# Spreading queries and keys ahead of the next raw weights in a hybrid decoder layer, with three weight splits moved

## The chip, the cores and the metric

The kernel runs on one core of a Trainium2 chip. The metric is device time in microseconds (us) for one execution of the whole layer. TensorE is called PE, VectorE DVE, ScalarE ACT, GpSimd POOL and SyncE SP, as in the profile. Before the change the median of 3 runs is 604.84 us (604.68 to 605.78).

## What is computed

One decoder layer on 512 tokens with 1024 channels, float32 throughout. The input projection feeds a pooling mixer (u) and block-sparse attention with 8 heads of 64 (q, k, v); then the output projection, a gated MLP with a short convolution, and an embedding gate:

```python
h = rms_norm(x, g_mix_pre[i])
proj = h @ w_in[i]
u, q, k, v = jnp.split(proj, [D_POOL, D_POOL + D_ATTN, D_POOL + 2 * D_ATTN], axis=-1)
y_pool = pool_mixer(u, w_pool[i], pool_scale[i])
y_attn = moba_attention(q, k, v, rel_bias)       # heads split off; own block and past blocks
y = jnp.concatenate([y_pool, y_attn], axis=-1) @ w_out[i]
x = x + rms_norm(y, g_mix_post[i])
h = rms_norm(x, g_ffn_pre[i])
x = x + rms_norm(conv_ffn(h, w_up[i], conv_w[i], conv_b[i], w_down[i]), g_ffn_post[i])
x = x + (p[i] @ w_ple[i]) * jax.nn.sigmoid(x @ w_ple_gate[i])
```

With 512 tokens, blocks of 256 and three past blocks to choose, every query sees all earlier keys, so the kernel computes plain causal attention.

## The kernel before

Every float32 product is made of three matmuls (`mm3`, lines 224 to 226) on operands that are split into a high and a low part: low times high, high times low, high times high. A weight therefore passes through four steps in the class `_Weights`. SP loads a chunk of 1 MB into one of two raw buffers (`load`, lines 110 and 118). A chunk holds two pieces; for each piece ACT casts the high part (`wh`, line 147) and DVE subtracts it from the raw data (`wl`, line 148). `W.ahead(n)` puts the splits of the next pieces into the program at the place where it is called, until n pieces beyond those already used are split. As soon as both pieces of a chunk are split, the load of the chunk two further on is put into SP's queue at that place.

The pieces in the order of their use: 0 to 3 the value weights, 4 and 5 the query weights of the first two pairs of heads (q0, q1), 6 and 7 their key weights (k0, k1), 8 and 9 pooling inputs u0 and u1, 10 to 13 q2, k2, q3, k3, 14 and 15 u2 and u3, 16 to 23 the output projection W_out. Chunk c holds the pieces 2c and 2c + 1.

`project` makes one projection of 24 matmuls and then calls `W.ahead(n)`. `query(hp)` projects the queries of a pair of heads and writes the high and low parts (lines 415 and 416) into the buffer `QK`. `key(hp)` does so for the keys (lines 229 and 230, the helper `split`). From `QK`, SP copies both parts into the operands of two single heads, `ST[0]` and `ST[1]`, in the trace the tiles q and k: four transfers of 128 KB for the queries (line 427) and four of 256 KB for the keys (line 434), two for each head. The next pair's projection can be written into `QK` only when these have landed. PE's scores of a head (line 444) need that head's q and k.

The attention is a hand-written order over the heads h = 0 to 6. For each h the program puts out one or two projections that fill PE (`fills`), then `transposes(h)` of the softmaxed scores L (line 471, evicted by ACT and DVE as `PT`), `scores(h + 1)` with the softmax of that head on DVE and ACT (lines 450 to 456, the last step being four multiplications on line 456), the copies of the next pair, and `values(h)` (line 491, whose result is taken from the bank that the first of the head's transposes used, and is evicted on lines 496 to 500). After head 6 PE makes parts of the output projection, `out_part(0, 0, ...)`, the tile y, with the input rows in the order 4, 5, 0, 1, 6, which are in the pieces 18, 18, 16, 16, 19. Then follow the transposes of head 7.

Every engine works through its instructions in program order, so the place of a call of `W.ahead` decides what waits behind a split on ACT and DVE and behind a load in SP's queue. The pooling inputs are summed on POOL (lines 512 to 518) beside the heads 0, 1, 5 and 6.

Of the kernel before, what the change touches and what calls it, by code (L numbers as in the profile page):

```python
# [17 lines left out]
F32 = mybir.dt.float32  # L18
# [12 lines left out]
H = 8  # L31
DH = 64
# [130 lines left out]
def hybrid_layer(ctx, tc, x, p, rel_bias, g_mix_pre, g_mix_post, g_ffn_pre, g_ffn_post, w_in, w_pool,  # L163
                 pool_scale, w_out, w_up, conv_w, conv_b, w_down, w_ple, w_ple_gate, onehot, out):
    nc = tc.nc
    act, dve, pool, pe, sp = nc.scalar, nc.vector, nc.gpsimd, nc.tensor, nc.sync
# [10 lines left out]
    def bank(name, tag="mm"):  # L177
        return psum.tile([P, 512], F32, tag=tag, name=name, bufs=banks[tag])


    W = _Weights(nc, wts)
# [33 lines left out]
    for i in GATE:  # L215
        if i in (1, 2, 3):
            row, n = {1: (0, 0), 2: (KG, 0), 3: (KG, 1)}[i]
# [4 lines left out]
    def mm3(o, st, mv, first, last, more=False):  # L222

        pe.matmul(o, st[1], mv[0], start=first, stop=False, skip_group_check=more)  # L224
        pe.matmul(o, st[0], mv[1], start=False, stop=False, skip_group_check=more)  # L225
        pe.matmul(o, st[0], mv[0], start=False, stop=last, skip_group_check=more)  # L226

    def split(pair, src):
        act.copy(pair[0], src)
        dve.tensor_sub(pair[1], src, pair[0].bitcast(F32))  # L230
# [37 lines left out]
    def h_moving(k, half=None):  # L268
        part = slice(0, NT) if half is None else slice(2 * half, 2 * half + 2)
        return [q[:, part, k, :] for q in hT]  # L270
# [104 lines left out]
    ps = bank("rows", "pt")  # L375
# [23 lines left out]
    def project(name, tag="mm", n=3):  # L399
        w = W.take()  # L400
        ps = bank(name, tag)
        for k in range(KD):
            mm3(ps, [q[:, k, :] for q in w], h_moving(k), k == 0, k == KD - 1)
        W.ahead(n)
        return ps
# [4 lines left out]
    QK = ap2.tile([P, 4, S], F32R, name="qk")  # L410
    ST = [[ap2.tile([P, S], F32R, name=f"q_{e}"), ap2.tile([P, 2, S], F32R, name=f"k_{e}")] for e in range(2)]

    def query(hp):
        ps = project(f"q{hp}")
        act.mul(QK[:, 0, :], ps, -(DH ** -0.5))
        dve.scalar_tensor_tensor(QK[:, 3, :], ps, -(DH ** -0.5), QK[:, 0, :].bitcast(F32), op0=ALU.mult,
                                 op1=ALU.subtract)

    def key(hp):
        ps = project(f"k{hp}")  # L420
        split([QK[:, 1, :], QK[:, 2, :]], ps)

    def spread_queries():

        for e in range(2):
            for a in range(2):
                sp.dma_start(ST[e][0][a * DH:(a + 1) * DH].bitcast(F32),
                             QK[e * DH:(e + 1) * DH, 0 if a == e else 3, :].bitcast(F32))

    def spread_keys():  # L430

        for e in range(2):
            for a in range(2):
                sp.dma_start(ST[e][1][a * DH:(a + 1) * DH].bitcast(F32), QK[e * DH:(e + 1) * DH, 1:3, :].bitcast(F32))

    place = {3: (0, 0, 768), 2: (1, 0, 384), 0: (1, 384, 0), 1: (2, 0, 128)}

# [38 lines left out]
    def moving(q, j):  # L476
        if j < 3:
            o = (P, P + 512, P + 896)[j]
            return q[:, o:o + (NT - j) * P]
        return q.rearrange("p (a b) -> p a b", b=P)[:, 0::10, :]  # L480

    def values(h):
        hp, e = divmod(h, 2)
        ps = bank(f"o{h}", "pt")
        for c in range(2):
            for j in range(NT):
                o = ps[:, min(j, 2) * P:]
                if j == 3:
                    o = o.rearrange("p (a b) -> p a b", b=P)
                w = V[:, j, hp, e].rearrange("p a d -> p (a d)")  # L490
                pe.matmul(o, w, moving(PT[c], j), start=j == 0 and c == 0, stop=j == NT - 1 and c == 1)  # L491
        rows = slice(e * DH, (e + 1) * DH)
        other = slice((1 - e) * DH, (2 - e) * DH)
        hi, lo = (q[rows, 4 + hp, :] for q in yT)
        t = ap2.tile([P, S], F32, tag="t", name=f"t{h}", bufs=1)
        act.copy(t[rows, :], ps[other, :])
        act.copy(hi, ps[rows, :])
        d = ap2.tile([P, S], F32, tag="d", name=f"d{h}", bufs=1)
        dve.tensor_sub(d[rows, :], ps[rows, :], hi.bitcast(F32))
        dve.tensor_add(lo, d[rows, :], t[rows, :])  # L500
# [3 lines left out]
    def pool_in(g):  # L504

        w = 2 << g
        ps = project(f"u{g}", n=4 if g == 3 else 3)
        act.copy(ub[0][:, 16:], ps)  # L508
        src = ub[0]
        for lvl in range(g + 1):  # L510
            nxt = ub[1 + lvl % 2]
            pool.tensor_tensor(out=nxt[:, 16:], in0=src[:, 16:], in1=src[:, 16 - (1 << lvl):16 + S - (1 << lvl)],  # L512
                               op=ALU.add)
            src = nxt
        pool.tensor_tensor(out=src[:, 16:16 + w], in0=src[:, 16:16 + w], in1=inv_count[:, :w], op=ALU.mult)
        pool.tensor_scalar(src[:, 16 + w:], src[:, 16 + w:], 1.0 / w, None, op0=ALU.mult)
        pooled[g] = ap2.tile([P, S], F32, tag="pd", name=f"pd{g}", bufs=2)
        pool.tensor_tensor(out=pooled[g], in0=src[:, 16:], in1=ub[0][:, 16:], op=ALU.subtract)
# [6 lines left out]
    def pool_out(g, tag="mm"):  # L525
        mp = bank(f"mix{g}", tag)
        mm3(mp, [q[:, g, :] for q in wp], pooled[g], True, True)
        act.mul(yT[0][:, g, :], mp, pscale[:, g:g + 1])
        dve.scalar_tensor_tensor(yT[1][:, g, :], mp, pscale[:, g:g + 1], yT[0][:, g, :].bitcast(F32),
                                 op0=ALU.mult, op1=ALU.subtract)  # L530
# [4 lines left out]
    def y_stationary(t, k):  # L535
        return [q[:, k, t * P:(t + 1) * P] for q in yT]

    yb = {}
    part = (4, 5, 0, 1, 6)
    query(0)  # L540
    spread_queries()
    query(1)
    key(0)
    spread_keys()
    key(1)
    split(wp, wpool)
    scores(0)
    fills = {0: [lambda: pool_in(0)], 1: [lambda: pool_in(1)],
             2: [lambda: query(2), lambda: pool_out(0)],
             3: [lambda: key(2), spread_keys, lambda: query(3), lambda: pool_out(1)],  # L550
             4: [lambda: key(3)], 5: [lambda: pool_in(2)],
             6: [lambda: pool_in(3)]}
    after = {1: lambda: pool_mid(0), 2: lambda: pool_mid(1), 6: lambda: pool_mid(2)}
    for h in range(H - 1):
        for f in fills[h]:
            f()
        transposes(h)
        scores(h + 1)
        if h in (0, 2, 4):
            spread_queries()  # L560
            if h != 2:
                spread_keys()
        values(h)
        if h in after:
            after[h]()

# [76 lines left out]
    for k in range(2):  # L643
        ps = bank(f"trp{k}", "pt")
# [137 lines left out]
    u = 0  # L782
    for fb in range(1, NF // 2):
        for post in (gate_post, value_post):
            for f in (2 * fb, 2 * fb + 1):
                ps = project(f"{post.__name__[:4]}{f}", tags[u % 5])
# [5 lines left out]
                else:  # L792
                    k, step = divmod(u - 2 * NK, 3)
# [36 lines left out]
    for g, (i, ks) in enumerate(GROUPS):  # L830
        m_next()
        w = W.take()
# [238 lines left out]
```

## Time and profile before

| | |
|---|---|
| median of 3 runs | 604.84 us |
| the profiled execution, its own time | 605.41 us |
| its span from first to last instruction | 603.6 us |
| PE busy | 588.9 us, 98% of the span |
| DVE, ACT, POOL busy | 424.0, 292.6, 234.8 us |
| PE's share of the chain that ended last | 92% |
| mean granted PE clock | 0.99 of full speed |

In the page's 40 slices of 15.1 us PE is busy in nine tenths or more of all but a few. The exceptions that lie in the attention are one slice of six tenths near 68 us, with a granted clock of seven tenths, and one of eight tenths near 143 us, with a clock of eight tenths. The list of PE's waits and the timelines around these two places tell what PE waited for.

### The profile page before, as it was taken

How to read it: one execution, taken by the hardware profiler on the slowest of the kernel's cores; microseconds unless marked ns; L12 is line 12 of the kernel's file. 1: busy time of each engine (PE TensorE's matmuls, PEld its weight loads, DVE VectorE, ACT ScalarE, POOL GpSimd, SP SyncE). 2: the span in 40 equal slices, each digit the busy share in tenths (PEclk: the TensorE clock that was granted, in tenths of full speed). 3: DMA queues.
4: the chain of work that ended last, by engine and by line, in shares of the span. 5: the costliest groups of instructions: out<-in, count | busy, mean ns of one | idle time of the engine just before them, and what ended most of it. 6: DMA issues, size and time to landing. Idle time of an engine off the chain costs nothing.

```text
span 603.6 us, 7483 instructions
## 1 busy us (share of the span) xinstructions
PE 588.9 (98%) x2752; PEld 489.5 (81%) x2752; DVE 424.0 (70%) x556; ACT 292.6 (48%) x476; POOL 234.8 (39%) x236
## 2 busy tenths in 40 slices
PE   9999699998999999999999999999999999999996
PEld 5887588887888998888888888888888878888885
DVE  4643278688468857868656658868787686878985
ACT  6432267566264534425334334444646565866461
POOL 2300050037213739998820787584240000012930
PEclk9999799998999999999999999999999999999999
DMA  8676563551642297998972565786655575752974
GB/s 296 199 268 181 130 175 104 157 159 69 245 139 71 79 390 269 344 356 287 375 269 69 210 208 210 259 287 218 206 170 185 191 270 184 262 193 72 346 242 176
DMA packets 68012, 128.57 MB, mean 213 GB/s; under 512 B 4115, under 2 KB 35439, under 8 KB 66568
## 3 DMA queue, kind: packets, MB, share of 16 engines
q1 hardware_dynamic: 58392, 88.69, 45.3%
q0 software_dynamic: 9584, 39.41, 17.3%
q8 instruction: 21, 0.34, 0.2%
q14 instruction: 15, 0.12, 0.1%
HBM read 97.65 MB, written 26.76 MB: 206 GB/s over the span
## 4 chain that ended last, share of the span: by engine, by line
PE 92%; DVE 2%; DMA 2%; ACT 1%; issue 1%; SPq 0%; POOL 0%; DVEq 0%; ACTq 0%; POOLq 0%
PE gate L224 6%; PE valu L224 6%; PE gate L226 6%; PE valu L226 6%; PE gate L225 6%; PE valu L225 6%; PE d L224 6%; PE d L226 5%; PE d L225 5%; PE y L226 2%; PE y L224 2%; PE y L225 2%; PE g L226 2%; PE g L225 2%; PE g L224 2%; PE o L491 2%
## 5 line engine op out<-in xcount | busy, mean ns | idle before, releaser
L148 DVE TENSOR_TENSOR wl<-raw,wh 128x1024 fp32r<-128x1024 f32 (+1 forms) x118 | 156.9, 1336 | 23.1 <-ACT wh L147 22.6
L147 ACT CAST wh<-raw 128x1024 fp32r<-128x1024 f32 (+1 forms) x118 | 118.7, 1021 | 23.4 <-DMA raw<-in_w_up 7.1
L741 POOL TENSOR_TENSOR b<-b 128x512 f32<-128x512 f32 x60 | 94.9, 1591 | 13.4 <-DMA b<-in_w_down 10.8
L224 PE MATMUL gate<-hT,wl 128*128 128x512 f32 x160 | 62.3, 389 | 0.0
L225 PE MATMUL gate<-hT,wh 128*128 128x512 f32 x160 | 62.3, 389 | 0.0
L226 PE MATMUL gate<-hT,wh 128*128 128x512 f32 x160 | 62.2, 389 | 0.0
L224 PE MATMUL valu<-hT,wl 128*128 128x512 f32 x160 | 62.2, 389 | 0.0
L225 PE MATMUL valu<-hT,wh 128*128 128x512 f32 x160 | 62.2, 389 | 0.0
L226 PE MATMUL valu<-hT,wh 128*128 128x512 f32 x160 | 62.2, 389 | 0.0
L224 PE MATMUL d<-wh,ml 128*128 128x512 f32 x154 | 60.0, 390 | 0.7 <-DVE ml L230 0.7
L225 PE MATMUL d<-wl,mh 128*128 128x512 f32 x154 | 59.9, 389 | 0.0
L226 PE MATMUL d<-wh,mh 128*128 128x512 f32 x154 | 59.9, 389 | 0.0
L512 POOL TENSOR_TENSOR u<-u 128x512 f32<-128x512 f32 x10 | 12.3, 1228 | 83.9 <-ACT u L508 83.4
L254 POOL TENSOR_SCALAR rd<-msd 128x1 f32<-128x1 f32 x4 | 3.4, 859 | 106.5 <-ACT M L249 106.4
L673 ACT ACTIVATE c<-gate,cols 128x512 f32<-128x512 f32 x20 | 15.5, 773 | 58.4 <-PE gate L226 58.4
L685 ACT ACTIVATE sq<-sq 128x512 f32<-128x512 f32 x22 | 13.9, 632 | 47.7 <-DVE sq L684 47.7
L674 DVE SCALAR_TENSOR_TENSOR c<-gate,cols,c 128x511 f32<-128x511 f32 x20 | 14.9, 745 | 29.7 <-ACT c L673 29.7
L226 PEld LDWEIGHTS gate<-hT,wh 128*128 128x128 f32 x160 | 30.0, 188 | 6.3
L226 PEld LDWEIGHTS valu<-hT,wh 128*128 128x128 f32 x160 | 30.0, 188 | 6.3
L225 PEld LDWEIGHTS valu<-hT,wh 128*128 128x128 f32 x160 | 30.0, 188 | 6.2
L224 PEld LDWEIGHTS valu<-hT,wl 128*128 128x128 f32 x160 | 30.0, 188 | 6.2
L225 PEld LDWEIGHTS gate<-hT,wh 128*128 128x128 f32 x160 | 30.0, 188 | 6.2
(241 smaller groups left out, 1360.2 us busy)
## 6 DMA issues: line engine op xcount, KB each, us to landing
raw<-in_w_up SPq DMA_DIRECT2D x22, 1024.0 KB, 7.4
b<-in_w_down POOLq DMA_DIRECT2D x22, 512.0 KB, 8.5
tsum<-b POOLq DMA_DIRECT2D x11, 1024.0 KB, 5.8
raw<-tsum SPq DMA_DIRECT2D x20, 512.0 KB, 5.4
raw<-in_w_down SPq DMA_DIRECT2D x15, 512.0 KB, 4.8
raw<-in_w_in SPq DMA_DIRECT2D x8, 512.0 KB, 5.7
raw<-in_w_in SPq DMA_DIRECT2D x4, 1024.0 KB, 5.8
k<-qk SPq DMA_DIRECT2D x16, 256.0 KB, 4.7
```

Source lines behind the costliest of these rows:

```text
L147: self.nc.scalar.copy(pair[0], view)
L148: self.nc.vector.tensor_sub(pair[1], view, pair[0].bitcast(F32))
L224: pe.matmul(o, st[1], mv[0], start=first, stop=False, skip_group_check=more)
L225: pe.matmul(o, st[0], mv[1], start=False, stop=False, skip_group_check=more)
L226: pe.matmul(o, st[0], mv[0], start=False, stop=last, skip_group_check=more)
L254: pool.tensor_scalar(r, ms, add, None, op0=ALU.add)
L491: pe.matmul(o, w, moving(PT[c], j), start=j == 0 and c == 0, stop=j == NT - 1 and c == 1)
L512: pool.tensor_tensor(out=nxt[:, 16:], in0=src[:, 16:], in1=src[:, 16 - (1 << lvl):16 + S - (1 << lvl)], op=ALU.add)
L673: act.activation(c0, pg, AF.Identity, bias=cw[:, 3, f:f + 1], scale=cw[:, 2, f:f + 1])
L674: dve.scalar_tensor_tensor(c0[:, 1:], pg[:, :S - 1], cw[:, 1, f:f + 1], c0[:, 1:], op0=ALU.mult, op1=ALU.add)
L685: act.activation(sq, sq, AF.Tanh, scale=GELU_A * GELU_C)
L741: pool.tensor_tensor(out=b[:, o, :], in0=b[:, i0, :], in1=b[:, i1, :], op=ALU.subtract)
```

## The change

`query` and `key` get a flag `spread_now`. With it the projection calls `W.ahead(0)`, and only when the eviction and the copies of the pair have been put into the program does `W.ahead(3)` follow. So the copies stand in SP's queue before the load of the next chunk, and the eviction stands on ACT and DVE before the splits of the next pieces. It is used for q0, k0 and k2. The function `spread` replaces the two separate ones; where it copies queries and keys in one call (at h = 0 and 4), it does all four transfers of the first head and then those of the second. Last, the projection that splits one piece more than usual is that of u2 (at h = 5) in place of that of u3 (at h = 6), and `W.ahead(4)` after `values(6)` splits the piece that is left.

```diff
-    def query(hp):
-        ps = project(f"q{hp}")
+    def query(hp, spread_now=False):
+        ps = project(f"q{hp}", n=0 if spread_now else 3)
         act.mul(QK[:, 0, :], ps, -(DH ** -0.5))
         dve.scalar_tensor_tensor(QK[:, 3, :], ps, -(DH ** -0.5), QK[:, 0, :].bitcast(F32), op0=ALU.mult,
                                  op1=ALU.subtract)
-
-    def key(hp):
-        ps = project(f"k{hp}")
+        if spread_now:
+            spread("q")
+            W.ahead(3)
+
+    def key(hp, spread_now=False):
+        ps = project(f"k{hp}", n=0 if spread_now else 3)
         split([QK[:, 1, :], QK[:, 2, :]], ps)
-
-    def spread_queries():
+        if spread_now:
+            spread("k")
+            W.ahead(3)
+
+    def spread(what):
+
 
         for e in range(2):
-            for a in range(2):
-                sp.dma_start(ST[e][0][a * DH:(a + 1) * DH].bitcast(F32),
-                             QK[e * DH:(e + 1) * DH, 0 if a == e else 3, :].bitcast(F32))
-
-    def spread_keys():
-
-        for e in range(2):
-            for a in range(2):
-                sp.dma_start(ST[e][1][a * DH:(a + 1) * DH].bitcast(F32), QK[e * DH:(e + 1) * DH, 1:3, :].bitcast(F32))
+            src = slice(e * DH, (e + 1) * DH)
+            for w in what:
+                for a in range(2):
+                    dst = ST[e][w == "k"][a * DH:(a + 1) * DH]
+                    cs = slice(1, 3) if w == "k" else 0 if a == e else 3
+                    sp.dma_start(dst.bitcast(F32), QK[src, cs, :].bitcast(F32))
...
-        ps = project(f"u{g}", n=4 if g == 3 else 3)
+        ps = project(f"u{g}", n=4 if g == 2 else 3)
...
-    query(0)
-    spread_queries()
+    query(0, True)
     query(1)
-    key(0)
-    spread_keys()
+    key(0, True)
     key(1)
...
-             3: [lambda: key(2), spread_keys, lambda: query(3), lambda: pool_out(1)],
+             3: [lambda: key(2, True), lambda: query(3), lambda: pool_out(1)],
...
         if h in (0, 2, 4):
-            spread_queries()
-            if h != 2:
-                spread_keys()
+            spread("q" if h == 2 else "qk")
         values(h)
+        if h == H - 2:
+            W.ahead(4)
```

SP's queue from the first copies on, before (the number after a name is that of its chunk, head or piece; the x2 of a raw chunk are its two pieces, that of q and k the two transfers for one head):

```order
L110 DMA raw5_453<-in_w_in 128x8x128 x2
L427 DMA q_0_410<-qk_409 64x512 x2
L427 DMA q_1_412<-qk_409 64x512 x2
L110 DMA raw6_522<-in_w_in 128x8x128 x2
L434 DMA k_0_411<-qk_409 64x1024 x2
L434 DMA k_1_413<-qk_409 64x1024 x2
L118 DMA raw7_619<-in_w_in 128x8x256
L427 DMA q_0_410<-qk_409 64x512 x2
L427 DMA q_1_412<-qk_409 64x512 x2
L434 DMA k_0_411<-qk_409 64x1024 x2
L434 DMA k_1_413<-qk_409 64x1024 x2
```

and the same queue with the change:

```order
L438 DMA q_0_410<-qk_409 64x512 x2
L438 DMA q_1_412<-qk_409 64x512 x2
L110 DMA raw5_459<-in_w_in 128x8x128 x2
L438 DMA k_0_411<-qk_409 64x1024 x2
L438 DMA k_1_413<-qk_409 64x1024 x2
L110 DMA raw6_528<-in_w_in 128x8x128 x2
L118 DMA raw7_619<-in_w_in 128x8x256
L438 DMA q_0_410<-qk_409 64x512 x2
L438 DMA k_0_411<-qk_409 64x1024 x2
L438 DMA q_1_412<-qk_409 64x512 x2
L438 DMA k_1_413<-qk_409 64x1024 x2
```

The first queries now stand ahead of chunk 5 and the first keys ahead of chunk 6; behind chunk 7 the first head's keys stand before the second head's queries.

DVE around the transposes of head 6 before (PT is the eviction of the transposes, d and yT that of the values, wl18 and wl19 the low parts of W_out's pieces):

```order
L456 TENSOR_SCALAR L6_1204<-L6_1204,m6_1205 128x256
L499 TENSOR_TENSOR d5_1231<-o5_1219,yT0_89 64x512
L500 TENSOR_TENSOR yT1_90<-d5_1231,t5_1228 64x512
L148 TENSOR_TENSOR wl18_1260<-raw9_966,wh18_1259 128x1024
L148 TENSOR_TENSOR wl19_1264<-raw9_966,wh19_1263 128x1024
L230 TENSOR_TENSOR PT1_415<-pt6_0_1278,PT0_414 128x512
```

With the change wl18 stands one head earlier, on DVE before the eviction of the transposes of head 5:

```order
L504 TENSOR_TENSOR yT1_90<-d4_1132,t4_1129 64x512
L148 TENSOR_TENSOR wl17_1161<-raw8_824,wh17_1160 128x1024
L148 TENSOR_TENSOR wl18_1167<-raw9_966,wh18_1166 128x1024
L230 TENSOR_TENSOR PT1_415<-pt5_0_1178,PT0_414 128x512
L230 TENSOR_TENSOR PT1_415<-pt5_1_1185,PT0_414 128x384
```

and wl19 later, on DVE behind the softmax of head 7 and the eviction of the values of head 6:

```order
L460 TENSOR_SCALAR L7_1302<-L7_1302,m7_1303 128x384
L460 TENSOR_SCALAR L7_1302<-L7_1302,m7_1303 128x128
L460 TENSOR_SCALAR L7_1302<-L7_1302,m7_1303 128x256
L503 TENSOR_TENSOR d6_1329<-o6_1317,yT0_89 64x512
L504 TENSOR_TENSOR yT1_90<-d6_1329,t6_1326 64x512
L148 TENSOR_TENSOR wl19_1333<-raw9_966,wh19_1332 128x1024
```

In front of the eviction of head 6 no split is left. PE's own order is unchanged.

## Rows read from the trace of the kernel before

**Rows 1.** PE's waits: engine, line waited for: us in total, times, longest us
```profile
PE s L444 <- issue: 5.0, 2, 4.7
PE o L491 <- DVE PT L230: 2.1, 1, 2.1
```
**Rows 2.** PE's timeline, 56 to 86 us: start, us, instruction, count [idle before <- releaser]
```profile
56.72 0.50 PE L224 MATMUL k<-hT,wl 128*128 128x512 f32 x1 [0.38 <-DVE qk L416]
...
67.16 2.68 PE L444 MATMUL s<-k,q 128*128 128x512 f32 x8 [4.67 <-issue]
...
76.56 1.25 PE L471 MATMUL pt<-ident,L 128*128 128x128 f32 x10
77.57 1.53 PE L444 MATMUL s<-k,q 128*128 128x512 f32 x8
78.94 1.46 PE L491 MATMUL o<-PT,V 128*128 128x512 f32 x8
80.23 0.40 PE L224 MATMUL u<-hT,wl 128*128 128x512 f32 x1
...
85.70 1.25 PE L471 MATMUL pt<-ident,L 128*128 128x128 f32 x10
```
**Rows 3.** Windows: us, busy us of each engine, granted PE clock, DMA share, GB/s
```profile
67.10:72.70 5.60, 5.54 (x16) 4.70 (x17) 2.79 (x9) 1.96 (x5) 0.00 (x0) 0.50 0.14 31
...
144.40:147.80 3.40, 3.40 (x13) 2.91 (x12) 2.07 (x10) 2.33 (x9) 3.18 (x4) 0.50 0.79 306
```
**Rows 4.** SP's queue timeline: start, us of issuing, transfer, count
```profile
58.16 1.00 SPq L110 DMA_DIRECT2D raw<-in_w_in  x2
59.27 4.39 SPq L434 DMA_DIRECT2D k<-qk  x4
...
107.50 3.13 SPq L434 DMA_DIRECT2D k<-qk  x4
```
**Rows 5.** DMA issues from 59.2 to 63.7 us: transfer, KB, median us to landing
```profile
k<-qk SPq DMA_DIRECT2D x4, 256.0 KB, 6.7
```
**Rows 6.** DMA issues from 107.4 to 110.7 us
```profile
k<-qk SPq DMA_DIRECT2D x4, 256.0 KB, 4.5
```
**Rows 7.** ACT's timeline, evictions of q1 and k1
```profile
55.34 0.60 ACT L415 ACTIVATE qk<-q 128x512 fp32r<-128x512 f32 x1 [8.25 <-DMA q<-qk]
...
69.29 0.59 ACT L229 CAST qk<-k 128x512 fp32r<-128x512 f32 x1 [10.98 <-DMA k<-qk]
```
**Rows 8.** DVE's timeline, low part of k0 and end of the softmax of head 0
```profile
58.05 0.68 DVE L230 TENSOR_TENSOR qk<-k,qk 128x512 fp32r<-128x512 f32 x1
...
74.38 1.27 DVE L456 TENSOR_SCALAR L<-L,m 128x512 f32<-128x512 f32 x4
```
**Rows 9.** DVE's timeline, heads 5 and 6: pieces 17 and 19, softmax of head 6
```profile
129.82 1.21 DVE L148 TENSOR_TENSOR wl<-raw,wh 128x1024 fp32r<-128x1024 f32 x1
...
136.27 2.20 DVE L456 TENSOR_SCALAR L<-L,m 128x512 f32<-128x512 f32 x4
...
141.09 2.06 DVE L148 TENSOR_TENSOR wl<-raw,wh 128x1024 fp32r<-128x1024 f32 x1
```
**Rows 10.** POOL's timeline, sums of u2
```profile
131.02 3.27 POOL L512 TENSOR_TENSOR u<-u 128x512 f32<-128x512 f32 x3 [39.10 <-ACT u L508]
```
**Rows 11.** ACT's timeline, high parts of pieces 18 and 19
```profile
137.26 2.00 ACT L147 CAST wh<-raw 128x1024 fp32r<-128x1024 f32 x2
```
**Rows 12.** PE's timeline, heads 5 to 7
```profile
130.16 1.25 PE L471 MATMUL pt<-ident,L 128*128 128x128 f32 x10
...
132.53 1.46 PE L491 MATMUL o<-PT,V 128*128 128x512 f32 x8
...
139.30 1.25 PE L471 MATMUL pt<-ident,L 128*128 128x128 f32 x10
...
143.93 2.33 PE L491 MATMUL o<-PT,V 128*128 128x512 f32 x8 [2.09 <-DVE PT L230]
...
150.33 1.37 PE L471 MATMUL pt<-ident,L 128*128 128x128 f32 x10
```

## Prediction

> **What bounds the kernel now.** The page gives PE 98% of the span and 92% of the chain, so a change pays only where PE waits or runs at a low clock. I read PE's waits first: within the attention only two are large, 4.7 us before a scores group on line 444 and 2.1 us before values on line 491 [rows 1]. PE's timeline places them. The first is before scores(0): PE is idle from 62.49 to 67.16 [rows 2]. The second is before values(6), up to 143.93 [rows 12]. The windows behind both show a granted clock of 0.50, which is 1.2 of 2.4 GHz [rows 3]. So each wait is paid twice. From 67.16 to 76.56 PE needs 9.40 us for scores (at full clock 77.57 to 78.94, 1.37) and 24 matmuls (80.23 to 85.70, 5.47) [rows 2]: 2.56 lost to the clock. From 143.93 to 150.33 it needs 6.40 us [rows 12] for values (78.94 to 80.23, 1.29) and 15 matmuls (15/24 of 5.47, 3.42): 1.69 lost. With PE's 0.38 before k1 [rows 2] and the 0.3 that is left of the 5.0 in rows 1 (scores(2)), the attention holds 4.67 + 2.56 + 2.09 + 1.69 + 0.38 + 0.3 = 11.7 us, the most that could be won.
>
> Why scores(0) wait: SP issues the two raw transfers of chunk 6 at 58.16 and the keys' four only from 59.27 [rows 4], and these take 6.7 us to land [rows 5]; the later four at 107.50, with no raw transfer ahead of them, take 4.5 [rows 6]. The same keys also hold ACT: the eviction of k1 waits 10.98 us, to 69.29, for the last copy, and q1's waits 8.25 for the queries [rows 7]. Values(6) wait for the eviction of the transposes, which on DVE stands behind the low parts of pieces 18 and 19.
>
> **The change part by part.** No instruction or transfer is added or removed; all is order.
>
> *Queries of q0 ahead of chunk 5.* The splits of k0 and k1 move behind q0's eviction. From the end of q0 PE has 5.47 us of q1 before it needs k0; the eviction takes ACT 0.60 and DVE about 0.7 and k0's split some 1.0 (half of rows 11) and 1.21 (rows 9), done by about 2.9. The cover is 2.6 us, so the cost is nothing. The copies land earlier, q1's eviction no longer waits, and PE's 0.38 before k1 goes. Chunks 5 and 6 load some microseconds later, but their first splits come on ACT ahead of k1's eviction at the earliest, or a head later, so that is hidden too.
>
> *Keys of k0 ahead of chunk 6.* k0's matmuls end at 56.34 (56.72 less 0.38). ACT 0.59, DVE 0.68 [rows 7, 8] and 0.1 of hand-over put SP's first issue at 57.7 instead of 59.27. The first head's second copy is issued 0.5 later and lands 4.5 after that, 62.7; scores(0) start at 62.75 instead of 67.16, a wait of about 0.6 against 62.1 (62.49 less 0.38). That is 1.7 times 0.38, which did not lower the clock, so I take it at full. PE then has u0 done at 62.75 + 1.37 + 5.47 = 69.6, which was 76.56.
>
> *What is late next: the softmax of head 0.* Transposes(0) need it, and on ACT and DVE it stands behind k1's eviction, which needs all four copies to have landed. In the undisturbed case the four issues take 3.13 [rows 4], so the last starts between 1.8 and 3.13 after the first and lands between 64.0 and 65.3; I take 64.5, near the early end, because the last issue is itself the end of the 3.13. ACT starts at 64.6, 4.7 before its 69.29 [rows 7]; the softmax, done at 75.65 [rows 8], is done at 70.95. Transposes(0) start at 71.0 instead of 76.56: **5.55 won** (4.75 to 6.05), with a new PE wait of 1.4.
>
> *The clock after this wait.* A wait of 0.38 cost no clock, one of 2.09 did. 1.4 is nearer to 2.09, and transposes and not long matmuls follow: I take the 1.7 of the later place: **1.7 lost** (0 to 1.7). Scores(2), with their keys now third and fourth behind chunk 7, lose their wait: **0.3 won**.
>
> *Piece 18 split at head 5.* ACT has room; on DVE the split starts at 131.03 (129.82 + 1.21) and pushes the eviction of transposes 5. At head 6 values start 0.78 after the last split's end (141.09 + 2.06 = 143.15, to 143.93). If this one takes 1.21 it ends at 132.24, and values(5) start at 133.0 instead of 132.53, 0.5 late; if 2.06 as at 141.09, at 133.87, 1.35 late [rows 9, 12]. POOL's sums begin at 131.02 [rows 10], the same moment, so neither row is nearer: **0.9 lost**, the middle.
> The trace has 2.06 beside POOL's sums and 1.21 without [rows 9, 10]. The Trainium skill (SBUF — State Buffer, "Who interferes with whom") says why: a DVE instruction with two SBUF inputs and a GpSimd one that reads SBUF share a port by an exclusive lock, and the second to start is blocked for the whole of the first. By that rule, with POOL first, the split waits for one sum (3.27 / 3 = 1.09) and values(5) come 1.6 late; the whole sum below would shrink from 0.85 to 0.15.
>
> *Piece 19 behind values(6).* I count from the start of transposes 6 at 139.30; transposes 7 come 11.03 later [rows 12]. Without the two splits values(6) start at +2.4 (1.01 and 1.37), which wins the 2.09 and its 1.69 for the moment. The tile y starts at +3.7 and after 12 matmuls (2.73) needs piece 19 at +6.4. Its low part stands on DVE behind the softmax of head 7. Head 5 to 6 gives the time: the last multiplications start 136.27 − 130.16 = 6.11 after the transposes and take 2.20 beside POOL or 1.27 alone [rows 8, 9, 12], so they end at +7.4 to +8.3, say 8.0; the evictions of values(6), two of 0.7, end at +9.4, the split (1.21) at +10.6. Its high part is on ACT at +8.1 (137.26 + 1.0 − 130.16) [rows 11], so one matmul slips in between. PE waits 4.0 us in all, and transposes 7 come at +11.1: **0.1 lost** (0.5 won if all is short; 1.2 lost with 8.3 and 2.06). A wait of 4.0 lies between 2.09 and 4.67, which lost 1.7 and 2.6 to the clock: **2.3 lost** (1.7 to 2.6); the clock that is won at values(6) is paid here again.
>
> **The sum.** 5.55 − 1.7 + 0.3 − 0.9 − 0.1 − 2.3 = 0.85 us won. The profiled execution took 605.41 (span 603.6, the rest before and after), so it would take 604.56; it lies 0.57 above the median of 604.84, from which I predict 604.84 − 0.85 = **604.0**. A measurement of this kernel tells 0.2%, 1.2 us, from no change; 0.85 is within it.
>
> **The rivals.**
> 1. *The clock holds after transposes(0), or the small terms fall short.* For it: 1.4 is less than the 2.09 that lowered the clock. Against it: transposes follow at once, as they preceded the 2.09. The time: 604.0 − 1.7 = 602.3; with piece 18 at its short end 601.9. Chance 0.38.
> 2. *Piece 19 does not hold PE*, because its split is done by +6.4. Then transposes 7 wait only for the softmax at +8.0: 3.1 won there and no 2.3, so 604.0 − 5.4 = 598.6. Against it: DVE's order puts 6.11 + 1.27 + 1.4 + 1.21 = 10.0 before it even at its shortest. Chance 0.05.
> 3. *Slower: piece 19 comes later than I think.* The place is DVE between the softmax of head 7 and the split. POOL makes the four sums of u3 there; if a sum delays the multiplications and another the split, and the copies of k0 land late as well, the split ends near +13 instead of +10.6. Each microsecond later is one lost: from +11.45 the whole gain is gone, from +12.7 the kernel is slower by more than 1.2. At +13, 604.0 + 2.4 = 606.4. For it: 2.20 and 2.06 in rows 9; against it: POOL is mostly done by then. Chance 0.12.
> 4. *The order in SP's queue does not matter*: the keys take 6.7 to land whatever stands ahead, for instance because copies from half the partitions are slow. Then the last lands at 66.7, transposes(0) start 2.2 later than I think, 606.2. Against it: 4.5 in rows 6. Chance 0.05.
>
> **How the numbers follow.** My forecast, within 0.2%, has 0.40. Faster is rivals 1 and 2, 0.43; slower is rivals 3 and 4, 0.17. The forecast's own range with the bounds of its terms is 602.6 to 605.4. The range that should hold 8 in 10 runs from 601.4 (rival 1 with short terms; rival 2 left out) to 605.9 (into rival 3; its end and rival 4 left out).
>
> **What would show it.** Right: SP's keys issued near 57.7 and landing in about 4.5; scores(0) near 62.8; a new wait of 1 to 2 us before transposes(0) with DVE's softmax as its end; then a window at a clock of 0.50; no wait at values(6); 0.5 to 1.4 us at values(5); waits in y before its 13th and 14th matmul, for ACT and DVE's piece 19, about 4 us in all, with a low clock behind. Wrong: no wait before transposes(0), so that the gain is nearer to 7; no wait within y; or scores(0) still above 64.

## The result, and the profile after

The changed kernel takes **600.42 us** (median of 4 runs, 600.02 to 600.69) against 604.96 of the kernel before on the same chip (604.68 to 605.78, 4 runs): a ratio of 0.9922, with a 95% interval of 0.9905 to 0.9939. A second measurement, below, gives 601.66 and 0.9948 (0.9936 to 0.9961). So it is 3.3 to 4.5 us faster. I had predicted 604.0, a gain of 0.85, with a range down to 601.4: wrong, by too little gain. The second measurement lies just inside that range, but its gain of 3.3 is still four times the forecast. The profiled execution took 600.02, with a span of 598.2.

PE's waits after the change (us in total, times, longest us; the four largest of those that lie in the stretch of the change):

```profile
PE y L225 <- DVE wl L148: 2.1, 1, 2.1
PE pt L475 <- DVE L L460: 1.6, 1, 1.6
PE y L224 <- ACT wh L147: 1.6, 1, 1.6
...
PE s L448 <- DMA k<-qk: 0.4, 1, 0.4
```

The 4.7 before scores and the 2.1 before values of [rows 1] are gone; the new waits stand where the prediction put them, before transposes(0) and twice within y. PE's timeline after (start, us, instruction, idle before it and releaser):

```profile
60.23 1.54 PE L448 MATMUL s<-k,q 128*128 128x512 f32 x8 [0.43 <-DMA k<-qk]
...
68.86 1.46 PE L475 MATMUL pt<-ident,L 128*128 128x128 f32 x10 [1.63 <-DVE L L460]
...
79.81 1.51 PE L448 MATMUL s<-k,q 128*128 128x512 f32 x8 [0.34 <-issue]
...
122.58 1.25 PE L475 MATMUL pt<-ident,L 128*128 128x128 f32 x10
...
125.29 1.55 PE L495 MATMUL o<-PT,V 128*128 128x512 f32 x8 [0.18 <-DVE PT L230]
132.15 1.25 PE L475 MATMUL pt<-ident,L 128*128 128x128 f32 x10
...
140.29 0.50 PE L224 MATMUL y<-wh,yT 128*128 128x512 f32 x1 [1.55 <-ACT wh L147]
...
142.86 0.51 PE L225 MATMUL y<-wl,yT 128*128 128x512 f32 x1 [2.07 <-DVE wl L148]
...
143.60 2.33 PE L475 MATMUL pt<-ident,L 128*128 128x128 f32 x10
...
149.61 0.40 PE L224 MATMUL mix<-p,wp 128*128 128x512 f32 x1
```

These answer to [rows 2] and [rows 12]: scores(0) at 60.23 (67.16), transposes(0) at 68.86 (76.56), transposes 6 at 132.15 (139.30). Behind the two places the windows show (us, busy us of each engine, granted PE clock, DMA share, GB/s):

```profile
68.80:72.40 3.60, 3.54 (x24) 3.25 (x25) 3.48 (x7) 1.51 (x4) 3.21 (x3) 1.00 0.23 40
143.20:146.60 3.40, 3.40 (x15) 3.00 (x14) 1.43 (x4) 1.54 (x3) 1.65 (x4) 0.50 0.76 263
```

After the wait before transposes(0) the clock stays at full speed; after those in y it is halved, 1.2 of 2.4 GHz. SP's queue and ACT's timeline show why scores(0) come earlier:

```profile
55.73 3.13 SPq L438 DMA_DIRECT2D k<-qk  x4
58.96 2.57 SPq L110 DMA_DIRECT2D raw<-in_w_in  x2
```

```profile
51.17 0.60 ACT L415 ACTIVATE qk<-q 128x512 fp32r<-128x512 f32 x1 [4.16 <-DMA q<-qk]
...
62.70 0.59 ACT L229 CAST qk<-k 128x512 fp32r<-128x512 f32 x1 [5.83 <-DMA k<-qk]
```

The keys are issued at 55.73 ahead of the raw chunk (59.27 behind it in [rows 4]). Their median time to landing is 3.7 us in the list of DMA issues (6.7 in [rows 5]); k1's eviction waits 5.83 instead of 10.98 [rows 7].

**An earlier start that is not the change's.** In this execution the first query matmul starts at 37.87, in that of before at 39.86, and the value matmuls ahead of it differ only in duration. One line of each timeline, first of before, then of after:

```profile
12.75 0.63 PE L225 MATMUL v<-wl,hT 128*128 128x512 f32 x1
...
39.86 0.39 PE L224 MATMUL q<-hT,wl 128*128 128x512 f32 x1
```

```profile
12.19 0.40 PE L225 MATMUL v<-wl,hT 128*128 128x512 f32 x1
...
37.87 0.39 PE L224 MATMUL q<-hT,wl 128*128 128x512 f32 x1
```

0.63 is the duration that the matmuls of u0 have before the change in the window at 0.50 of [rows 3], 0.40 that at full clock. So I read this as a clock that rose later in the one execution than in the other. The rows don't show it: the column of the granted clock has 1.00 here, in before too (windows as above):

```profile
10.00:15.00 5.00, 5.00 (x11) 2.56 (x12) 3.81 (x6) 4.97 (x7) 0.78 (x2) 1.00 1.03 385
```

That the matmuls were slower is measured; that the clock was the cause is argued from the durations alone. The first experiment asks whether the later start belongs to the kernel.

### The profile page after: what moved, and what is told of

The parts are those of the page before. It is cut to its first block, busy times and chain, and to the rows that moved or that the text cites. A ratio compares the mean times of both kernels' runs of the same rounds, so it can differ in the third digit from the quotient of the medians.

```text
span 598.2 us, 7479 instructions
## 1 busy us (share of the span) xinstructions
PE 584.1 (98%) x2752; PEld 485.1 (81%) x2752; DVE 425.4 (71%) x556; ACT 293.1 (49%) x476; POOL 236.5 (40%) x236
## 4 chain that ended last, share of the span: by engine, by line
PE 89%; DVE 4%; ACT 3%; issue 1%; DMA 1%; POOL 0%; SPq 0%; DVEq 0%; ACTq 0%; POOLq 0%
PE gate L225 6%; PE valu L225 6%; PE gate L226 6%; PE valu L226 6%; PE gate L224 6%; PE valu L224 6%; PE d L224 6%; PE d L226 6%; PE d L225 6%; PE y L225 2%; PE y L226 2%; PE y L224 2%; PE g L225 2%; PE g L224 2%; PE g L226 2%; PE o L495 1%
## 5 line engine op out<-in xcount | busy, mean ns | idle before, releaser
L148 DVE TENSOR_TENSOR wl<-raw,wh 128x1024 fp32r<-128x1024 f32 (+1 forms) x118 | 159.0, 1356 | 23.8 <-ACT wh L147 23.3
L224 PEld LDWEIGHTS gate<-hT,wl 128*128 128x128 f32 x160 | 30.0, 188 | 6.3
```

What stands on the lines that cost most here:

```text
L148: self.nc.vector.tensor_sub(pair[1], view, pair[0].bitcast(F32))
```

## The experiments

The theories. **A**: the moved copies bring the gain and the moved splits cost, as the prediction had it, with the clock's share put wrong. **L**: the earlier start is luck of one execution. **P**: it belongs to the changed kernel. **S**: in the kernel before an early start is lost again in the waits for the copies, while the change keeps it. **Q** and others are stated where they are tried. All kernels were compared with the kernel before on the same chip (605.0 to 605.3).

The table splits each profiled execution at three starts on PE's timeline: the first query matmul; transposes 6, behind all moved copies and piece 18; and the first mix matmul behind transposes 7 and y. Copies and piece 18 act in the second column of numbers, piece 19 in the third. What follows the mix matmul is the same 448.5 to 449.5 us in all.

| kernel | us, median (runs) | ratio, 95% interval | first query at | to transposes 6 | on to mix |
|---|---|---|---|---|---|
| before, first profile | 604.84 (3) | | 39.86 | 99.44 | 15.69 |
| before_again | 605.27 (1) | | 37.86 | 101.29 | 15.69 |
| after | 600.42 (4) | 0.9905 to 0.9939 | 37.87 | 94.28 | 17.46 |
| after_again | 601.66 (6) | 0.9936 to 0.9961 | 38.41 | 94.70 | 17.42 |
| spread_only | 598.93 (4) | 0.9885 to 0.9914 | 39.86 | 93.97 | 15.69 |
| splits_only | 607.37 (5) | 1.0032 to 1.0057 | 37.83 | 101.71 | 17.42 |
| keys_only | 600.62 (6) | 0.9902 to 0.9939 | 38.44 | 96.13 | 15.69 |
| queries_only | 601.28 (6) | 0.9917 to 0.9946 | 38.34 | 96.83 | 15.71 |
| scores_first | 599.16 (6) | 0.9881 to 0.9915 | 37.88 | 92.34 | 18.58 |
| one_each | 596.36 (4) | 0.9834 to 0.9874 | 38.73 | 94.15 | 13.01 |
| both_mended | 593.78 (4) | 0.9796 to 0.9826 | 37.87 | 92.62 | 12.51 |
| late_before | 608.99 (6) | 1.0039 to 1.0089 | 39.95 | 104.46 | 15.68 |
| late_after | 604.62 (12) | 0.9974 to 0.9996 | 39.95 | 95.82 | 17.48 |

**before_again and after_again** run both kernels once more, with nothing edited.

> The kernel before once more, for a second profile. In the first two profiles PE's first query matmul starts at 39.86 us (before) and 37.87 us (after), though no instruction ahead of it differs: the value matmuls from 12 us on ran at the low clock until about 18 us before the change, and from 10 us on at the full clock after it. Theory L (luck): where the clock rises at the start differs from execution to execution, so this profile may show the first query matmul at either place, and the total moves by up to 2 us with it. Theory P (property): it belongs to the kernel, and this one shows 39.9 us again. Both: the wait before scores(0) near 4.7 us and the one before values(6) near 2.1 us again.

> The changed kernel once more. Theory L: the first query matmul starts anywhere from 37.5 to 40 us; the five rounds against before spread accordingly and their mean gain lies between 3 and 5 us. Theory P: 37.9 us in this profile too, and a gain of 4.5 us in every round. Both: waits of 0.4 before scores(0), 1.6 before transposes(0), 1.6 and 2.1 inside y, and a low clock only behind the last.

In before_again the first query matmul starts at 37.86, as early as in the change: theory L holds, the start varies between executions of one kernel. (The value matmuls shorten from 0.63 to 0.39 at another time in each profile: they are short from the first one near 11 us here and in after, from near 15 in after_again and only from near 18 in before. The Trainium skill, TensorE: Matmul & The Clock Gate, Part 1 on the HAM clock gate, says that what sets this clock runs freely and isn't reset by a kernel's start, so that the moment of the change varies. The durations fit that, though they differ by more than the half microsecond that the Trainium skill names there, and the granted clock, 1.00 in this stretch, doesn't show it.) Yet the span is nearly that of the first profile, 603.5 against 603.6. PE's timeline of before_again shows where the 2.0 us went:

```profile
56.59 0.50 PE L224 MATMUL k<-hT,wl 128*128 128x512 f32 x1 [2.25 <-DVE qk L416]
66.71 1.71 PE L444 MATMUL s<-k,q 128*128 128x512 f32 x8 [2.79 <-issue]
...
87.27 1.52 PE L444 MATMUL s<-k,q 128*128 128x512 f32 x8 [1.60 <-issue]
...
143.78 1.55 PE L491 MATMUL o<-PT,V 128*128 128x512 f32 x8 [2.10 <-DVE PT L230]
150.18 1.37 PE L471 MATMUL pt<-ident,L 128*128 128x128 f32 x10 [1.40 <-DVE L L456]
```

The wait before k1 grew from 0.38 to 2.25, that at scores(2) from 0.36 to 1.60, and scores(2) start at 87.27, where the first profile has 87.32:

```profile
87.32 1.52 PE L444 MATMUL s<-k,q 128*128 128x512 f32 x8 [0.36 <-issue]
```

In these two the start of scores(2) doesn't follow PE's earlier start, so something else sets it; I take it to be the copies. One more thing is to be read here. The wait at values(6) is 2.10, as in [rows 12], but the window behind it stays at full clock:

```profile
143.80:147.20 3.40, 3.40 (x17) 2.98 (x18) 2.49 (x10) 1.91 (x7) 3.10 (x5) 1.00 0.85 289
```

The 1.7 that [rows 3] lost to the clock there is not won, though: a wait of 1.40 for the softmax of head 7 takes its place, and transposes 7 start 11.03 after transposes 6 in both.

**spread_only and splits_only** make the two halves of the change apart: the copies moved, the splits as before; and the splits moved, the copies as before.

```diff
 # spread_only: the change with
-        ps = project(f"u{g}", n=4 if g == 2 else 3)
+        ps = project(f"u{g}", n=4 if g == 3 else 3)
-        if h == H - 2:
-            W.ahead(4)
 # splits_only: the kernel before with
-        ps = project(f"u{g}", n=4 if g == 3 else 3)
+        ps = project(f"u{g}", n=4 if g == 2 else 3)
+        if h == H - 2:
+            W.ahead(4)
```

> Only the copies of queries and keys moved; the splits of the pieces 18 and 19 stay before values(6). Theory A (the parts add up as in the trace of the change): from the first query matmul to transposes(6) this takes 94.1 us, as with the change less 0.2, against 99.4 before, and the 2.1 us wait at values(6) is back with its low clock; total 1.8 to 2.0 us below the changed kernel. Rival B (the splits moved are what makes room, the copies alone win less): total at or above the changed kernel.

> Only the splits moved; the copies stay behind the raw chunks. Theory A: waits of 1.6 and 2.1 us inside y replace the 2.1 us at values(6), with a low clock behind them; from transposes(6) to the product mix of pool group 2 it takes about 17.5 us against 15.7 before, and the total is 1.8 to 2.0 us above the kernel before (apart from the start). Rival B: at or below the kernel before.

Theory A holds in the main. The copies alone win 6.0 us (604.98 to 598.93), the splits alone lose 2.4 (to 607.37), and the sum, 3.6, lies within what the change wins. Two of its details didn't come: the splits were to lose 1.8 to 2.0, and the 2.1 at values(6) in spread_only was to have a low clock behind it. spread_only is also the fair test of the prediction's first half, because its execution starts at 39.86 like that of before. Its waits and timeline:

```profile
PE pt L475 <- DVE L L460: 3.0, 2, 1.6
PE o L495 <- DVE PT L230: 2.1, 1, 2.1
```

```profile
62.23 1.54 PE L448 MATMUL s<-k,q 128*128 128x512 f32 x8 [0.44 <-DMA k<-qk]
...
70.90 1.46 PE L475 MATMUL pt<-ident,L 128*128 128x128 f32 x10 [1.65 <-DVE L L460]
```

Scores(0) at 62.23 and transposes(0) at 70.90 were forecast at 62.75 and 71.0. Behind both the 1.65 and the 2.1 at values(6) its windows are at full clock:

```profile
70.90:74.50 3.60, 3.60 (x24) 3.30 (x25) 3.48 (x6) 1.45 (x4) 3.27 (x3) 1.00 0.26 40
138.50:142.00 3.50, 3.50 (x18) 3.03 (x19) 2.47 (x10) 2.03 (x7) 3.20 (x5) 1.00 0.93 296
```

The third column says what the splits cost: 17.42 to 17.48 for y with piece 19 behind values(6), 15.68 to 15.71 with the splits where they were. Scores_first (18.58) stands out: its granted clock is 0.50 from 140.1 to 146.7, about twice as long as in after. The second column adds some 0.4 for piece 18 (101.71 against 101.29 at nearly the same start).

**keys_only and queries_only** move only the first keys, or only the first queries, ahead of their raw chunk.

```diff
 # keys_only: the kernel before with
-    def key(hp):
-        ps = project(f"k{hp}")
+    def key(hp, now=False):
+        ps = project(f"k{hp}", n=0 if now else 3)
         split([QK[:, 1, :], QK[:, 2, :]], ps)
+        if now:
+            spread_keys()
+            W.ahead(3)
...
-    key(0)
-    spread_keys()
+    key(0, True)
 # queries_only: the same in query, with spread_queries and query(0, True)
```

> The kernel before with one edit: key(0) copies its keys before its raw chunk is ordered (the queries, the later copies and the splits stay as before). Theory A (each raw transfer ahead of copies delays these copies by itself, and the keys' delay is the one that holds PE): scores(0) start near 62.8 instead of 67.2, the wait there is under 1.5, a new wait of 1 to 1.7 before transposes(0); the kernel takes 599.5 to 601.5 against 605.1 before, most of the 6.0 that all moved copies gave. The wait before k1 stays (0.4 to 2.3, by the start). Rival Q (the queries' copies are what counts, because k0's eviction waits behind q1's): scores(0) still near 66, and 603.5 or more.

> The kernel before with one edit: query(0) copies its queries before its raw chunk is ordered (keys, later copies and splits as before). Theory A: the wait before k1 goes (0.4 to 2.3 before), the wait at scores(0) stays 2.8 to 4.7 and its low clock with it, scores(0) start at 65 to 67; 603.5 to 605, at most 1.6 faster. Rival Q: scores(0) start below 64 and the kernel takes 599 to 601.5. Both edits' gains need not add up to 6.0: if keys alone give 4.5 and queries alone 1, the pair is additive; if each alone gives under 1.5, the one needs the other.

The keys alone win 4.5 us, as theory A expected (one of the six runs took 977.89 at a mean granted clock of 0.56; why is not known, and the median doesn't hang on it). The queries alone win 3.9, where A expected 1.6 at most: a miss, and rival Q is right that they count. Together the two should give 8.4, but all the moved copies give 6.0. The timelines of queries_only, ACT first, then SP and PE, show the way:

```profile
54.86 0.59 ACT L229 CAST qk<-k 128x512 fp32r<-128x512 f32 x1 [2.08 <-PE k L226]
```

```profile
54.06 0.99 SPq L110 DMA_DIRECT2D raw<-in_w_in  x2
56.20 3.42 SPq L437 DMA_DIRECT2D k<-qk  x4
```

```profile
62.81 2.68 PE L447 MATMUL s<-k,q 128*128 128x512 f32 x8 [2.54 <-DMA k<-qk]
```

With the queries landed early, ACT evicts q1 at 51.24 (55.34 in [rows 7]), the splits behind it come earlier, and so does the load that they free: raw chunk 6 is issued at 54.06 instead of 58.16 [rows 4]. It still stands ahead of the keys, whose landing takes 5.3, between 3.7 without it and 6.7. And k0's eviction, which stands behind q1's, waits only for PE and starts at 54.86 (56.77 in before), so the keys are issued at 56.20 instead of 59.27: 17.86 after the first query matmul, as in the change, where before has 19.41. So one delay had two causes in a row, and either edit removes most of it: scores(0) start at 62.44 with the keys alone, 62.81 with the queries alone, 60.23 in the change (24.0, 24.5 and 22.4 after the first query matmul; 27.3 in before). What my sum had at "nothing" (the queries of q0 ahead of chunk 5) is here worth most of the gain when it stands alone and, by difference, 1.5 on top of the keys (6.0 − 4.5), in which the later copies have a part that wasn't tried apart.

**scores_first** tests the prediction's step that k1's eviction holds the softmax of head 0.

```diff
-    def key(hp, spread_now=False):
+    def key(hp, spread_now=False, first=None):
         ps = project(f"k{hp}", n=0 if spread_now else 3)
+        if first:
+            first()
         split([QK[:, 1, :], QK[:, 2, :]], ps)
...
-    key(1)
+    key(1, first=lambda: scores(0))
     split(wp, wpool)
-    scores(0)
```

> The change with one edit: scores(0) and the softmax of head 0 stand on ACT and DVE ahead of k1's eviction. My step in the prediction (k1's eviction, which waits for the last copy of the keys, delays the softmax and so transposes(0)): the wait of 1.6 before transposes(0) goes, transposes(0) start 1.5 to 1.7 earlier after scores(0); 1.0 to 1.8 faster than the change (600.4 and 601.7), so 599 to 600. Rival (the softmax is late by its own length): the wait before transposes(0) stays over 1 and the time is that of the change within 0.6.

```profile
60.26 1.55 PE L450 MATMUL s<-k,q 128*128 128x512 f32 x8 [0.45 <-DMA k<-qk]
67.13 1.25 PE L477 MATMUL pt<-ident,L 128*128 128x128 f32 x10
```

On PE's timeline the wait before transposes(0) is gone: 6.87 after scores(0), which was 8.63 (68.86 − 60.23). The kernel takes 599.16, 1.3 to 2.5 less than the two measurements of the change. The step is right. The edit also puts the softmax ahead of the split of the pool weights, which wasn't tried apart; but that split delays DVE by only some 0.6 us (0.68 long, the next starts 0.60 behind it) of the 3.50 by which the softmax starts earlier there (61.03 instead of 64.53), and PE's wait was 1.63.

**one_each** asks whether the splits' cost is that of bunching: one more piece is split already at query(3), so that heads 4 to 6 split one each and nothing stands behind values(6).

```diff
-        ps = project(f"q{hp}", n=0 if spread_now else 3)
+        ps = project(f"q{hp}", n=0 if spread_now else 4 if hp == 3 else 3)
...
-        ps = project(f"k{hp}", n=0 if spread_now else 3)
+        ps = project(f"k{hp}", n=0 if spread_now else 4 if hp == 3 else 3)
...
-        ps = project(f"u{g}", n=4 if g == 2 else 3)
+        ps = project(f"u{g}", n=4 if g >= 2 else 3)
...
-        if h == H - 2:
-            W.ahead(4)
```

> The changed kernel with every projection from query(3) on splitting one piece further ahead, so that head 3 splits three pieces and the heads 4, 5 and 6 one each, and nothing is left behind values(6). Theory A (the split behind the softmax of head 7 holds PE, and two splits in one head hold it too): no wait above 0.5 us at values(5), values(6) or inside y; transposes(7) come 8.0 to 9.0 us after transposes(6) instead of 11.3 to 11.5, waiting only for their softmax; no low clock there. Total 596.5 to 598. Rival D (head 3 or the softmax of head 7 takes it all back): 599 or more.

```profile
132.88 1.25 PE L475 MATMUL pt<-ident,L 128*128 128x128 f32 x10
...
140.89 0.30 PE L475 MATMUL pt<-ident,L 128*128 128x128 f32 x1 [0.55 <-DVE L L460]
141.40 1.20 PE L475 MATMUL pt<-ident,L 128*128 128x128 f32 x9 [0.21 <-DVE L L460]
```

No wait is left at values(5), values(6) or in y. Transposes 7 start 8.0 after transposes 6, where before and the change need 11.03 and 11.45; they now wait for the softmax alone. 596.36 is 2.6 below spread_only.

**both_mended** puts one_each and scores_first together.

> one_each, and scores(0) with their softmax stand in the program ahead of the eviction of k1 and of the split of the pool weights, so that the softmax of head 0 no longer waits for the last copy of k0. Theory A (my step: k1's eviction, held by the copies, holds the softmax and this holds transposes(0)): the wait of 1.6 us before transposes(0) goes, 1.0 to 1.8 us below one_each. Rival: another wait of the same size comes up (values(0) or scores(1), or scores(2) for copies that now start later), 0 to 0.5 us below one_each.

It takes 593.78, a ratio of 0.9811 (0.9796 to 0.9826): 11.5 us below the kernel before on the same chip (605.26), and below every other kernel here. PE's waits in this stretch:

```profile
PE s L450 <- DMA k<-qk: 0.9, 2, 0.5
PE pt L477 <- DVE L L462: 0.7, 1, 0.7
```

and the windows from scores(0) to the end of the attention have no low clock:

```profile
60.00:100.00 40.00, 39.63 (x203) 33.62 (x204) 31.41 (x80) 27.31 (x62) 9.08 (x9) 1.00 0.56 148
100.00:200.00 100.00, 98.86 (x548) 85.19 (x547) 74.00 (x129) 54.47 (x113) 36.50 (x48) 1.00 0.44 138
```

The step from one_each, 2.6 us, is more than was expected of it. The table has 1.53 of it up to transposes 6 and 0.50 behind them.

**late_before and late_after** delay both kernels alike, to test theory S: 20 transposes, whose result nobody reads, stand ahead of query(0).

```diff
+    late = bank("late")
+    for _ in range(20):
+        pe.transpose(late[:, :P], ident, ident)
     query(0)
```

> The kernel before with 20 dummy transposes on PE ahead of the first query projection, about 2.0 us at full clock, as if the clock had risen late at the start. Theory S (slack): before the change the copies of q0 and k0 stand behind raw chunks whose times do not depend on PE, so a PE that comes earlier only waits longer (second profile of before: query matmuls 2.0 us earlier, wait before k1 2.25 instead of 0.38, scores(0) only 0.45 earlier). The 2.0 us vanish in these waits: scores(0) start within 0.7 us of 67.0, total +0.2 to +1.0 us against before. Rival N: nothing absorbs them, total +2.0.

> The changed kernel with the same 20 dummy transposes. Theory S: no wait ahead of scores(0) is left that could absorb them, scores(0) start 2.0 us later, total +1.5 to +2.2 us against the changed kernel (601.0 in the mean of its ten runs), so 602.5 to 603.2. Rival N: +2.0 as well, so it is the pair of kernels that tells: S wants the two additions to differ by more than 1 us.

S's numbers aren't met: late_before is 3.7 slower than the kernel before, late_after 3.0 to 4.2 slower than the change. The absorption itself is there, at scores(0), but another wait undoes it. PE's timeline of late_before and the window behind the second wait:

```profile
67.89 1.99 PE L444 MATMUL s<-k,q 128*128 128x512 f32 x8 [4.49 <-issue]
...
89.64 2.68 PE L444 MATMUL s<-k,q 128*128 128x512 f32 x8 [2.78 <-issue]
```

```profile
89.30:96.00 6.70, 6.36 (x20) 5.71 (x21) 3.30 (x14) 3.59 (x11) 2.42 (x2) 0.50 0.01 3
```

The start is 2.09 later than in before_again (39.95 against 37.86), scores(0) only 1.18 (67.89 against 66.71). But scores(2) wait 2.78, and the clock behind them is halved for the whole window: some 3.3 us more, an estimate from half of its 6.70. In late_after scores(2) wait 1.75 instead of 0.34. The keys of the second pair take 7.0 and 7.7 us to land in these two, 6.4 and 6.6 in before and after; why is open. So S is seen in single profiles, and this pair neither bears it out nor refutes it.

## Why the prediction was wrong

**Right, by its own steps.**
- *Keys ahead of chunk 6.* Scores(0) at 62.75 were forecast; 62.23 in spread_only, the execution with the same start.
- *What is late next.* Transposes(0) at 71.0 with a wait of 1.4, set by the softmax behind k1's eviction, were forecast; 70.90 with 1.65 in spread_only. 5.66 won against 5.55. scores_first shows that the cause is the right one.
- *Piece 19.* A wait for ACT and then one for DVE in y before its 13th and 14th matmul, 4.0 together, with transposes 7 at +11.1: after has 1.55 + 2.07 = 3.62 and +11.45. The split of piece 19 ends on DVE at +10.66 (141.60 + 1.21 − 132.15), forecast at +10.6:

```profile
138.33 1.66 DVE L460 TENSOR_SCALAR L<-L,m 128x512 f32<-128x512 f32 x4
...
141.60 1.21 DVE L148 TENSOR_TENSOR wl<-raw,wh 128x1024 fp32r<-128x1024 f32 x1
```

**The step that failed: the clock after this wait.** "1.4 is nearer to 2.09, and transposes and not long matmuls follow: I take the 1.7 of the later place." In the six profiles with that wait (after, after_again, spread_only, keys_only, one_each, late_after; 1.25 to 1.65 us) the clock behind it was 1.00. I had set a rate of exchange between waits and clock from single waits of one execution. The 2.09 itself is no certain loss: behind a wait of 2.09 to 2.13 at values(6) the clock is halved in before, from 1.4 us behind its start in queries_only (0.70 over the window), and full in before_again, late_before, spread_only and keys_only. And where it was full, nothing was won: transposes 7 then waited 1.39 or 1.40 for their softmax and came no earlier, so the 1.7 that I took from there was not even a price at its own place. That the clock holds was rival 1, which had 0.38; its time, 602.3, was still too high, in part by the first two terms of the list below.

This is what the profiles show. The runs without a trace give only their mean granted clock, and of the ten runs of the change it is 0.994 in three (all of the second measurement) and 0.996 or 0.997 in seven. So some executions have more or longer stretches at the low clock than the two profiled ones; whether one lies behind transposes(0) is not known.

**Terms that were mis-sized.**
- *Piece 18 at head 5*: 0.9 forecast, the middle between 0.5 and 1.35; about 0.4 measured. From transposes 5 to 6 it is 9.57 (132.15 − 122.58) against 9.14 [rows 12]. DVE and POOL after:

```profile
122.29 2.34 DVE L148 TENSOR_TENSOR wl<-raw,wh 128x1024 fp32r<-128x1024 f32 x2
```

```profile
123.44 4.33 POOL L516 TENSOR_TENSOR u<-u 128x512 f32<-128x512 f32 x3 [39.01 <-ACT u L512]
```

  DVE's two splits take 1.17 each, as alone; the sums on POOL, 3.27 in [rows 10], take 4.33 instead. So POOL paid for the meeting, and PE doesn't wait for POOL. By the rule that the prediction cited (the Trainium skill, SBUF — State Buffer, "Who interferes with whom") the one that starts second is held for the whole of the other. 1.06 more on POOL, all of it in the first sum (2.09, the other two 1.04 each), fits a split of 1.17 that came first; the version by which the sum comes first, 1.6 lost, didn't come about.
- *Piece 19 with the clock after it*: 0.1 + 2.3 = 2.4 forecast. Measured 1.77 (17.46 − 15.69): 0.42 until transposes 7, and 1.35 more from there to the mix matmul, with the low clock of 143.20 to 146.60 in it.
- *Scores(2)*: 0.3 was to be won; the wait stayed (0.34 in after, 0.41 in spread_only, 0.36 before).
- *Queries of q0 ahead of chunk 5*: put at nothing, because the later loads were hidden. So they were, but I overlooked that an earlier eviction of q1 also brings the next split, the next raw chunk and k0's eviction forward. Alone that is worth 3.9. It didn't spoil the sum: the keys' issue at 57.7 in the next step already took for granted that k0's eviction isn't held behind q1's, so the gain stood in the keys' term under the wrong name.

**The sum again.** Copies: 99.44 − 93.97 = 5.47 in two executions with the same start, where I had 5.55 − 1.7 + 0.3 = 4.15. Splits: 0.43 + 1.77 = 2.2, where I had 0.9 + 0.1 + 2.3 = 3.3. So 3.3 us instead of 0.85. The rest of the 5.4 between the two profiled spans is about the earlier start of 2.0. The start matters for the gain: of two executions that both start early, before_again and after, the second is 7.01 − 1.77 = 5.2 faster behind the first query matmul, each figure from a single pair of profiles. By the medians of the halves it is 6.0 − 2.4 = 3.6. The two measurements of the change lie 1.2 apart (600.42 and 601.66); the three runs at a mean clock of 0.994 may be a part of that, and the rest is not explained.

**The other rivals.** Piece 19 did hold PE (rival 2), its split came at +10.66 and not near +13 (rival 3), and the order in SP's queue mattered (rival 4): 3.7 us of landing with the raw chunk behind, 6.7 with it ahead.

## What to carry to other kernels

Transfers that a chain of work waits for belong ahead of bulk loads in their queue, and the loads' own triggers (splits, evictions) behind the chain's: here that is worth 6 us of 605, and the splits, spread one to a head, and the softmax ahead of an eviction that waits, bring 5 more. A low clock behind a short wait, seen in one execution, is not a price: look at the same place in a second execution, and ask whether the next wait would take back what a full clock gives. An earlier finish upstream is worth only what the next transfer's landing leaves of it.

## What the runs showed of the hardware

- Behind waits of 2.5 to 4.7 us of PE at scores(0) and scores(2) the clock fell in all the profiles that have one (before, before_again, splits_only, late_before, queries_only); behind single waits of up to 1.94 in none of the profiles; behind 2.09 to 2.25 sometimes: before k1 a 2.25 halved it in before_again, and the like in splits_only did not. The pair in y, 1.55 and 2.0 to 2.1 with one matmul between, lowered it in all five profiles that have it. The two windows behind k1, of before_again and of splits_only:

```profile
57.70:61.00 3.30, 3.30 (x9) 2.60 (x8) 2.04 (x3) 0.48 (x1) 0.00 (x0) 0.50 0.46 123
```

```profile
56.60:61.00 4.40, 4.40 (x19) 3.65 (x20) 2.96 (x3) 1.56 (x3) 0.00 (x0) 1.00 0.33 88
```

- The moment at which the value matmuls become short differs by some 7 us between executions (0.63 until then, 0.39 from there, from 11 to 18 us), and the start of the queries by 2.0. The granted clock reads 1.00 all through, so that it is the clock is argued and not shown.
- When DVE's splits and POOL's sums met, at head 5 only the sums were longer, 4.33 instead of 3.27 for three (4.29 to 4.34 in the five profiles with piece 18 there). At head 6 before the change both were: 2.06 instead of 1.21 for a split [rows 9], 6.29 for four sums where after has 4.66.
